# Weights and inputs laid out by the host as the chip wants them, and one scaling moved behind its load, in a two-layer hybrid decoder on eight cores

## The chip, the cores and the metric

The kernel runs on all 8 cores of one Trainium2 chip, one sequence of the batch per core. The metric is the device time of the slowest core, in microseconds (us). Most executions agree within 0.3%. Some fall into a slower state in which the cores of one die show a lower granted TensorE clock and the time is several per cent longer, whatever the kernel; those runs are left out of every comparison here, and only fast runs are compared with fast runs.

Engines are named as in the profile: PE is TensorE (matmuls and transposes), PEld its weight loads, DVE VectorE, ACT ScalarE, POOL GpSimd, SP SyncE. A kernel line is written L756.

## The reference, cut to what matters

```python
# D_MODEL 1024, BATCH 8, SEQ 2048, DEPTH 2, FFN_HIDDEN 2816, PLE_DIM 256
def even_mixer(x, w_in, w_out, conv_w, conv_b, ln_g, ln_b, pos):      # layer 0
    z = x @ w_in                                   # 1024 -> 5632
    q, k, v, u = jnp.split(z, [1536, 3072, 4608], axis=-1)
    ...                                            # rope on q, k; dilated window attention
    conv = conformer_conv(u, conv_w, conv_b, ln_g, ln_b)    # GLU, 31 taps, LN, SiLU
    return jnp.concatenate([attn, conv], axis=-1) @ w_out

def short_conv_mixer(x, w_in, conv_w, w_out): ...                     # layer 1

def reference(x, p, ...):
    for i in range(DEPTH):
        mix = even_mixer(...) if i % 2 == 0 else short_conv_mixer(...)
        x = layer_norm(DN_ALPHA * x + mix, ln_mix_g[i], ln_mix_b[i])
        x = layer_norm(DN_ALPHA * x + swiglu(x, ffn_w_in[i], ffn_w_out[i]), ln_ffn_g[i], ln_ffn_b[i])
        x = x + (p[i] @ ple_w_proj[i]) * jax.nn.sigmoid(x @ ple_w_gate[i])
    return x
```

All inputs are float32; the kernel computes its matmuls in bf16. A load from float32 in memory to a bf16 tile casts on the way, and in this kernel all of those are issued by POOL.

## The kernel before

`S.op`, `S.mm` and `S.dma` record an instruction with the tiles that it reads and writes; semaphores are derived from that. Every engine runs its own instructions in the order in which they were recorded.

Weights come through a ring of four tiles. A piece is 256 columns of a weight matrix, cut out of the row-major original in one or two loads:

```python
    def _wissue():
        while wq["issued"] < len(pieces) and wq["issued"] - 4 < wq["done"]:
            m = wq["issued"]
            i = m % 4
            fns = []
            for (src, co) in pieces[m]:
                n = src.shape[1]                                   # 128 or 256 columns
                fns.append(lambda e, src=src, co=co, n=n, i=i: e.dma_start(
                    out=ring[i][:, :, co:co + n], in_=src.rearrange("(kc p) n -> p kc n", p=128)))
            S.dma("pool", fns, ds_ring[i], writes=[r_ring[i]])
            wq["issued"] += 1
```

The start loads x by rows as float32, casts, transposes on PE, and after each four tiles of 128 tokens runs the GLU matmuls of the Conformer part for these 512 tokens. Two diagonal matrices for the convolution are built on POOL afterwards.

```python
    S.dma("sp", [... ropeC ..., ... ropeS ...], ds_misc, writes=[r_ropeC, r_ropeS])   # 2 MB
    for t in range(NT):
        S.dma("sp", [... x_tok[:, t, :] <- x_d[t * 128:(t + 1) * 128, :]], ...)
    ...
    for t in range(NT):
        if t + 2 < NT:
            p0_cast(t + 2)
        cb, r_cb = stg[t % 4]
        transpose_to(cb, r_cb, lambda t=t: xT[:, :, t * 128:(t + 1) * 128], r_xT[t // 4], 8,
                     "dve" if t % 2 == 0 else "act")
        if t % 4 != 3:
            continue
        ...                                        # GLU: 64 matmuls for this chunk
    # ... cut ...
    build_dg(0)
    build_dg(1)
```

The middle of the feed-forward part (four of the six groups of hidden columns). An output tile is 8 matmuls into PSUM and a DVE add that empties it:

```python
    def ffn_mid(l):
        S.dma("sp", [... lnp2 <- LN rows ...], ds_ln, writes=[r_lnp2])
        S.dma("pool", [... Wpg <- pwg_d[l] ..., ... Wpp <- pwp_d[l] ...], ds_ple, writes=[r_Wpg, r_Wpp])
        S.op("dve", lambda e: e.tensor_scalar_mul(out=Wpp[:], in0=Wpp[:], scalar1=0.5), rw=[r_Wpp])
        for t in range(NT):
            out_tile(0, t, False)
        for pi in range(1, len(FG) - 1):
            ...                                    # inproj tiles of group pi, 4 pieces
            load_wfo(l, pi + 1)
            for t in range(NT):
                out_tile(pi, t, False)
```

The tail is a software pipeline: round k works on tile k of the input projection, on tile k - 4 of the output, k - 5 of the layer norm, k - 6 of the transposes, k - 7 of the gate.

```python
    def ffn_tail(l, last, fill):
        for k in range(NT + 4 + 6):
            ...                                    # inproj(k % 4, k // 4)
            if ok(k - 4):
                out_tile(pi, k - 4, True)          # with LN statistics
            ln_apply(k - 5, lg, r_lnp2, lb, r_lnp2)
            if ok(k - 6):
                t = k - 6
                transpose_to(pbt[t % 2], r_pbt[t % 2], lambda t=t: pTt[t % 2][:], r_pTt[t % 2], 2, "dve")
                transpose_to(castt[t % 2], r_castt[t % 2], lambda t=t: x2T[t % 2][:], r_x2T[t % 2], 8, "dve")
            if ok(k - 5):
                p_load(l, k - 5)                   # 128 rows of p, 64 KB as bf16
            if ok(k - 7):
                p_main(l, k - 7)                   # x2T @ Wpg, tanh, pTt @ Wpp, gate, POOL add
            if ok(k - 5):
                cast_to(k - 5, castt[(k - 5) % 2], r_castt[(k - 5) % 2])       # ACT
            ...
```

The softmax here doesn't subtract the row's maximum and nothing guards it: scores larger than these inputs give would overflow.

## Time and profile before

| | before |
|---|---|
| median of 4 runs | 2335.0 us (2333.38 to 2335.57) |
| profiled execution, slowest core | 2333.9 us (core 3) |
| PE busy | 84% |
| DVE, POOL, ACT busy | 53%, 25%, 18% |
| granted PE clock, die 0 and die 1 | 0.938, 0.940 |
| software DMA packets | 154496 |

The chain of waits, the sums of the waits and the busy time by stretch are read in the prediction below. The two tails by stretch (columns: from:to, length, then busy time of PE, PEld, DVE, ACT and POOL with the number of instructions, PE clock, DMA share, GB/s):

```profile
1289.00:1512.00 223.00, 184.18 (x1018) 89.12 (x1017) 155.84 (x205) 57.91 (x65) 90.81 (x69) 0.93 0.12 15
2157.00:2334.00 177.00, 147.93 (x767) 69.55 (x765) 125.41 (x157) 39.39 (x44) 88.09 (x64) 0.94 0.18 54
```

Neither PE nor DVE fills these stretches, so they are held by waits between engines. The waits of PE from 2165 us to the end say which (us in all, times, longest):

```profile
PE ptb L455 <- DMA pbt<-p: 14.5, 6, 4.2
PE ptb L455 <- DVE x_tok L783: 6.9, 3, 2.7
PE ptb L455 <- ACT castt L500: 0.3, 1, 0.3
```

And the timeline at the head of this tail, where the first two tiles of the gate part come (start, length, engine, line, work, in brackets the idle time before it and what ended it):

```profile
2185.14 0.37 PE L455 MATMUL ptb<-ident,pbt 128*128 128x128 bf16 x2 [3.76 <-DMA pbt<-p]
...
2186.16 2.76 PE L774 MATMUL pd<-Wfo,hTf 128*128 128x512 bf16 x6
2193.13 0.37 PE L455 MATMUL ptb<-ident,pbt 128*128 128x128 bf16 x2 [4.21 <-DMA pbt<-p]
```

PE stands still for 8.0 us in all.

### The profile page before, as it was taken

Reading aid. Unit: us, or ns where it says so; the run is one execution under the profiler, and the core shown is the slowest. Engines: PE = TensorE matmul, PEld = TensorE weight load, DVE = VectorE, ACT = ScalarE, POOL = GpSimd, SP = SyncE. Lnnn points to the kernel's source line nnn. Section 1 sums busy time; section 2 is a strip of 40 time slices with the busy share of each in tenths; the row PEclk is TensorE's granted clock in tenths of the full one; section 3 lists DMA queues with packets and bytes.
Section 4 is the critical chain, followed back from the end, with each engine's and each line's share of the span. In section 5 each row is a group of like instructions: output and inputs, shape, how many; then the busy total and the mean of one; then the engine's idle time right before and its main releaser. Section 6 shows DMA issues by size and latency. Waiting matters only on the chain.

```text
span 2333.9 us, 27781 instructions; the slowest of 8 cores (2324.1 to 2333.9 us)
## 1 busy us (share of the span) xinstructions
PE 1950.2 (84%) x10046; PEld 939.2 (40%) x10046; DVE 1230.6 (53%) x1605; ACT 415.1 (18%) x629; POOL 586.9 (25%) x453
## 2 busy tenths in 40 slices
PE   3878787788853588699999897899897799999897
PEld 1434444345431243244444343444443344444443
DVE  1252665726735674333444676666883432444686
ACT  1203112231132221011001132211111011001122
POOL 1061633305410123010011254210332010100365
PEclk9999998999966799799999898999999899999899
DMA  9140201102045007352333003063217232232012
GB/s 191 33 47 12 28 9 20 18 11 28 10 55 162 0 1 90 46 54 25 40 41 41 4 8 32 22 80 38 29 18 87 39 46 28 37 40 32 23 62 79
DMA packets 163701, 97.30 MB, mean 42 GB/s; under 512 B 119280, under 2 KB 145904, under 8 KB 163312
## 3 DMA queue, kind: packets, MB, share of 16 engines
q0 software_dynamic: 154496, 63.97, 24.6%
q1 hardware_dynamic: 9072, 31.54, 4.2%
q8 instruction: 84, 1.38, 0.2%
q14 instruction: 49, 0.40, 0.1%
HBM read 151.08 MB, written 8.39 MB: 68 GB/s over the span
## 4 chain that ended last, share of the span: by engine, by line
PE 60%; DVE 18%; issue 8%; DMA 6%; ACT 5%; POOL 3%; DVEq 0%; SPq 0%; ACTq 0%; POOLq 0%
PE pd L750 24%; PE pd L774 12%; PE pd L943 6%; PE pd L853 4%; PE pd L630 3%; DMA x_tok<-x 2%; PE pd L736 2%; DVE rtmp L613 2%; DMA Wpp<-ple_w_proj 2%; DVE PT L661 2%; DVE rtmp L616 2%; DVE rtmp L610 2%; PE ptb L455 2%; DVE x_tok L492 1%; DVE UD L688 1%
## 5 line engine op out<-in xcount | busy, mean ns | idle before, releaser
L750 PE MATMUL pd<-xT,ring 128*128 128x512 bf16 x2816 | 620.6, 381 | 0.0
L750 PEld LDWEIGHTS pd<-xT,ring 128*128 128x128 bf16 x2816 | 275.8, 98 | 329.8 <-issue 6.4
L774 PE MATMUL pd<-Wfo,hTf 128*128 128x512 bf16 x1408 | 318.0, 385 | 47.6 <-DVE x_tok L779 47.6
L754 DVE TENSOR_TENSOR hTf<-pd,sgt 128x512 bf16<-128x512 f32 x176 | 121.7, 691 | 430.6 <-PE pd L750 407.2
L411 POOL DMA_DIRECT2D ring<-ffn_w_in x88 | 77.6, 890 | 665.5 <-PE pd L750 646.3
L753 ACT ACTIVATE sgt<-pd 128x512 f32<-128x512 f32 x176 | 104.7, 595 | 726.9 <-PE pd L750 726.9
L783 DVE TENSOR_TENSOR x_tok<-x_tok,pd 128x1024 f32<-128x1024 f32 x160 | 195.2, 1220 | 63.8 <-PE pd L774 54.9
L774 PEld LDWEIGHTS pd<-Wfo,hTf 128*128 128x128 bf16 x1408 | 139.0, 99 | 217.3 <-issue 56.5
L605 PE MATMUL pd<-xT,ring 128*128 128x512 bf16 x768 | 176.5, 384 | 30.8 <-DVE rtmp L616 29.0
L484 POOL TENSOR_SCALAR mvall<-mvall 128x1 f32<-128x1 f32 x64 | 64.6, 1009 | 465.3 <-DVE mvall L483 441.4
L943 PE MATMUL pd<-xT,ring 128*128 128x512 bf16 x768 | 170.7, 384 | 3.2 <-DMA ring<-odd_w_in 2.3
L620 POOL TENSOR_TENSOR qT<-rtmp,rtmp 128x512 bf16<-128x512 f32 x48 | 85.5, 1784 | 215.7 <-DVE rtmp L616 215.6
L661 DVE TENSOR_TENSOR PT<-PT,masks 128x256 bf16<-128x256 bf16 (+1 forms) x96 | 46.4, 483 | 161.3 <-ACT PT L658 161.3
L605 PEld LDWEIGHTS pd<-xT,ring 128*128 128x128 bf16 x768 | 72.9, 98 | 132.5 <-issue 54.7
L569 PE MATMUL pd<-hTc,dgb 128*128 128x512 bf16 x496 | 124.4, 387 | 0.0
L853 PE MATMUL pd<-Wpg,x2T 128*128 128x512 bf16 x512 | 123.2, 397 | 0.0
L455 PE MATMUL ptb<-ident,castt 128*128 128x128 bf16 x576 | 47.9, 233 | 80.6 <-ACT castt L500 54.1
L943 PEld LDWEIGHTS pd<-xT,ring 128*128 128x128 bf16 x768 | 75.3, 99 | 94.5 <-issue 7.8
L630 PE MATMUL pd<-ring,xT 128*128 128x256 bf16 x768 | 94.2, 284 | 22.2 <-DVE rtmp L616 22.2
L500 ACT ACTIVATE castt<-x_tok 128x1024 bf16<-128x1024 f32 x64 | 67.5, 1054 | 206.5 <-DVE x_tok L495 203.2
L869 POOL TENSOR_TENSOR x_tok<-x_tok,sigt 128x1024 f32<-128x1024 f32 x32 | 75.8, 2370 | 89.4 <-DVE sigt L867 72.0
L486 POOL TENSOR_TENSOR mvall<-mvall,cneg 128x1 f32<-128x1 f32 x64 | 95.3, 1490 | 9.5
(122 smaller groups left out, 2157.0 us busy)
## 6 DMA issues: line engine op xcount, KB each, us to landing
ring<-ffn_w_in POOLq DMA_DIRECT2D x88, 256.0 KB, 6.1
x_tok<-x SPq DMA_DIRECT2D x32, 512.0 KB, 6.6
ring<-even_w_in POOLq DMA_DIRECT2D x18, 512.0 KB, 7.8
Wfo<-ffn_w_out POOLq DMA_DIRECT2D x8, 1024.0 KB, 12.7
out<-x_tok SPq DMA_DIRECT2D x16, 512.0 KB, 2.7
Wpg<-ple_w_gate POOLq DMA_DIRECT2D x2, 2048.0 KB, 21.9
ring<-odd_w_in POOLq DMA_DIRECT2D x16, 256.0 KB, 7.9
Wfo<-ffn_w_out POOLq DMA_DIRECT2D x4, 768.0 KB, 9.8
```

Source lines behind the costliest of these rows:

```text
L455: fns = [lambda e, c=c, pt=pt: e.transpose(out=pt[:, c * 128:(c + 1) * 128], in_=src_bf[:, c * 128:(c + 1) * 128], identity=ident[:]) for ...
L486: S.op("pool", lambda e: e.tensor_tensor(out=mvall[:, t, 2:3], in0=mvall[:, t, 1:2], in1=cneg[:], op=ALU.pow), reads=[r_cneg], rw=[r_mvall ...
L569: fn = lambda e, tap=tap, bk=bk, j=j, tc=tc: e.matmul(bk, lhsT=dgb[j % 2][:, tap, :], rhs=hTc[:, j, tc * 512 + 2 + tap:tc * 512 + 2 + tap ...
L605: fns = [lambda e, d=d, bk=bk, w_=w_, h=h, tc=tc: e.matmul(bk, lhsT=w_[:, d, h * 128:(h + 1) * 128], rhs=xT[:, d, tc * 512:(tc + 1) * 512] ...
L630: fns = [lambda e, d=d, bk=bk, st0=st0, dil=dil, wv=wv: e.matmul(bk[:, 0:256], lhsT=xT[:, d, st0:st0 + 127 * dil + 1:dil], rhs=wv[:, d, :] ...
L750: S.mm([lambda e, d=d, bk=bk, o=o: e.matmul(bk, lhsT=slot[:, d, o:o + 128], rhs=xT[:, d, c * 512:(c + 1) * 512], start=(d == 0), stop=(d = ...
L753: S.op("act", lambda e: e.activation(out=sgt[k2][:], in_=bg, func=AF.Silu), reads=rg, writes=[r_sgt[k2]])
L754: S.op("dve", lambda e: e.tensor_tensor(out=hTf[:, fl, c * 512:(c + 1) * 512], in0=bu, in1=sgt[k2][:], op=ALU.mult), reads=ru + [r_sgt[k2] ...
L774: fns.append(lambda e, half=half, ff=ff: e.matmul(bD[:, half * 512:(half + 1) * 512], lhsT=hTf[:, ff, t * 128:(t + 1) * 128], rhs=Wfo[wb][ ...
L783: S.op("dve", lambda e: e.tensor_tensor(out=x_tok[:, t, :], in0=x_tok[:, t, :], in1=bD[:], op=ALU.add), reads=rD, rw=[r_xtok[t]])
L853: fns.append(lambda e, half=half, c=c: e.matmul(bG[:, half * 512:(half + 1) * 512], lhsT=x2T[k2][:, c, :], rhs=Wpg[:, c, half * 512:(half ...
L943: S.mm([lambda e, d=d, bk=bk, w_=w_, o=o: e.matmul(bk, lhsT=w_[:, d, o:o + 128], rhs=xT[:, d, c * 512:(c + 1) * 512], start=(d == 0), stop ...
```

## The change

Its intent is to have the host lay out what the chip otherwise rearranges, and to take three waits off the path:

- weights: 78 pieces, each packed by the host so that a partition's part is one contiguous run, one load instead of one or two;
- x a second time, transposed by the host, loaded with a cast straight into xT; rope tables only after it; one diagonal built at the start;
- p transposed by the host, 16 loads of 128 KB instead of 32 of 64 KB, no transposes of it on PE;
- Wpg, Wpp and their LN rows loaded after feed-forward group 1, the scaling by 0.5 done in group 3;
- the last two adds on DVE instead of POOL.

The other large weights (the output projections, the gate and the projection) are reordered by the host too, so that a partition's part is contiguous.

```diff
     def _wissue():
-        while wq["issued"] < len(pieces) and wq["issued"] - 4 < wq["done"]:
+        while wq["issued"] < min(len(PIECES), wq["lim"]) and wq["issued"] - 4 < wq["done"]:
             m = wq["issued"]
             i = m % 4
-            fns = []
-            for (src, co) in pieces[m]:
-                n = src.shape[1]
-                fns.append(... e.dma_start(out=ring[i][:, :, co:co + n], in_=src.rearrange(...)))
-            S.dma("pool", fns, ds_ring[i], writes=[r_ring[i]])
+            S.dma("pool", [lambda e, m=m, i=i: e.dma_start(out=ring[i][:], in_=wp_d[m])], ds_ring[i], writes=[r_ring[i]])
 ... cut: the loads of rope tables and of x by rows, casts and transposes at the start are removed ...
+    def xT_load(c):
+        S.dma("pool", [lambda e: e.dma_start(out=xT[:, :, c * 512:(c + 1) * 512], in_=xT_d[c])], ds_xT[c], writes=[r_xT[c]])
+    wq["lim"] = 1
+    _wissue()
+    xT_load(0)
+    wq["lim"] = len(PIECES)
     glu_slots = [wnext() for _ in range(4)]
+    for c in range(1, 4):
+        xT_load(c)
+    S.op("pool", ... dgb[1] = ident * ccw[:, 1, :] ...)
+    xT_landed = list(r_xT[3].ws.values())
 ... cut: GLU matmuls, unchanged ...
+    S.dma("sp", [... ropeC ..., ... ropeS ...], ds_misc, writes=[r_ropeC, r_ropeS], deps=xT_landed)
     build_dg(0)
-    build_dg(1)
     def ffn_mid(l):
-        S.dma("sp", [... lnp2 ...])
-        S.dma("pool", [... Wpg ..., ... Wpp ...], ds_ple, writes=[r_Wpg, r_Wpp])
-        S.op("dve", lambda e: e.tensor_scalar_mul(out=Wpp[:], in0=Wpp[:], scalar1=0.5), rw=[r_Wpp])
         for t in range(NT):
             out_tile(0, t, False)
 ... cut ...
             load_wfo(l, pi + 1)
+            if pi == 1:
+                S.dma("pool", [... Wpg ..., ... Wpp ...], ds_ple, writes=[r_Wpg, r_Wpp])
+                S.dma("sp", [... lnp2 ...])
+            if pi == 3:
+                S.op("dve", lambda e: e.tensor_scalar_mul(out=Wpp[:], in0=Wpp[:], scalar1=0.5), rw=[r_Wpp])
 ... cut: p_load takes two tiles at once from the transposed p ...
-        S.op("pool", lambda e: e.tensor_tensor(out=x_tok[:, t, :], in0=x_tok[:, t, :], in1=sg_[:], op=ALU.add),
+        S.op("dve" if l == 1 and t >= NT - 2 else "pool", lambda e: e.tensor_tensor(...),
 ... cut: in the tail ...
-                transpose_to(pbt[t % 2], r_pbt[t % 2], lambda t=t: pTt[t % 2][:], r_pTt[t % 2], 2, "dve")
                 transpose_to(castt[t % 2], r_castt[t % 2], lambda t=t: x2T[t % 2][:], r_x2T[t % 2], 8, "dve")
-            if ok(k - 5):
-                p_load(l, k - 5)
+            if ok(k - 5) and k % 2:
+                p_load(l, (k - 5) // 2)
 ... cut: the host code that packs and transposes ...
```

## The prediction

> **What bounds the kernel now.** I read the chain of waits first, because it names what ended last in each stage; then the waits, summed; then busy time by stretch, and the timeline where the two left a question. Columns of the chain: start, length (us), work.
>
> ```profile
> 7.34 18.29 DMA x_tok<-x
> ...
> 56.66 3.30 DMA x_tok<-x
> 63.81 3.46 PE pd L539 x8
> ...
> 129.06 6.82 POOL dgb L559
> ...
> 926.24 24.90 DMA Wpp<-ple_w_proj
> 953.20 25.09 PE pd L774 x104
> ...
> 1424.15 12.54 DMA pbt<-p
> ...
> 1797.02 22.48 DMA Wpp<-ple_w_proj
> ```
>
> Mostly the chain is PE matmuls (60% of the span by engine), but it leaves PE for a transfer at the start, once in each feed-forward stage, and often in the two tails. The waits (total us, times, longest) size this:
>
> ```profile
> PE ptb L455 <- DMA pbt<-p: 37.4, 12, 12.5
> ...
> DVE Wpp L828 <- DMA Wpp<-ple_w_proj: 52.2, 2, 27.3
> PE pd L774 <- DVE x_tok L779: 47.6, 2, 25.0
> ```
>
> The last two are one event. DVE multiplies Wpp by 0.5 as its first instruction of the stage, sits until the 2.6 MB of Wpg and Wpp have landed, and cannot empty PSUM; after three tiles PE stops. Busy time by stretch (core 3; PE, PEld, DVE, ACT, POOL, PE clock, DMA share, GB/s):
>
> ```profile
> 0.00:64.00 64.00, 22.00 (x129) 11.85 (x130) 9.54 (x18) 12.49 (x14) 8.80 (x17) 1.00 0.92 192
> 925.00:955.00 30.00, 5.02 (x20) 1.98 (x19) 3.77 (x4) 0.00 (x0) 1.96 (x3) 0.60 0.97 122
> 955.00:1290.00 335.00, 335.00 (x1546) 151.43 (x1545) 135.35 (x138) 35.82 (x60) 29.44 (x34) 1.00 0.34 35
> 1825.00:2170.00 345.00, 345.00 (x1600) 156.37 (x1599) 137.57 (x140) 38.21 (x64) 27.65 (x32) 1.00 0.28 33
> ```
>
> In the first 64 us the DMA engines are the bound (0.92 busy, PE 22 us). In 955 to 1290 and 1825 to 2170 PE is never idle, so faster weight loads are worth nothing there. So of the packing I count only the start; the rest of the gain comes from reordering.
>
> ```profile
> DMA packets 163701, 97.30 MB, mean 42 GB/s; under 512 B 119280, under 2 KB 145904, under 8 KB 163312
> ...
> q0 software_dynamic: 154496, 63.97, 24.6%
> ```
>
> The mean software packet writes 414 B and costs 24.6% x 2333.9 x 16 / 154496 = 59.5 ns of one engine.
>
> **What the Trainium skill says.** "DMA: Bandwidth & Descriptors", section "Why small descriptors are slow (HBM only)": each packet carries a fixed overhead. The trace agrees in direction: weight pieces with 256 B written per packet move about 90 GB/s per unit of DMA share, Wpg with 2 KB rows about 150 (932 to 951). Two rates give, as my estimate, t = 20.9 ns + 0.0963 ns per byte written; at 414 B that is 60.8, against 59.5 from the page. The same page, section "Anatomy of one DMA": a fixed cost of about 2 us a transfer; the 64 KB loads of p land in 2.4 us, so it agrees. "TensorE: Matmul & The Clock Gate", Part 1: a PE left idle for some 3.4 us restarts at half clock. It agrees: after the waits eight matmuls take 3.46 us, afterwards 1.73, so each long gap costs about 1.7 us more. "GPSIMD Engine Reference", section "Engine selection": two-input elementwise work is about 2x slower on GpSimd; here the final add takes 2.34 us on POOL and a like one 1.21 on DVE.
>
> **The change part by part.**
>
> 1. Start. Now 16 tiles of x are loaded as f32 beside 4.2 MB of weights in small packets and 2 MB of rope tables, cast, and transposed on PE with four breaks. The GLU matmuls start at 43.1 and end at 120.1. Afterwards x arrives transposed by casting loads, in the order piece 0, xT0, pieces 1 to 3, xT1 to xT3; the rope tables wait for xT3. By the estimate xT (1 KB rows written) moves 137 GB/s, 7.7 us a chunk, and a packed piece (4 KB rows if runs merge) 158 GB/s, 3.3 us. First issue at 3.07 as now, plus 2 fixed, plus 3.3 + 7.7: xT0 at 16.1. Pieces 1 to 3 at 19.4, 22.7, 26.0; xT1, xT2, xT3 at 33.7, 41.3, 49.0. A chunk of GLU is 64 matmuls in 13.8 us (four times 3.45), the first 1.7 more: it ends at 31.6, the second runs 33.7 to 47.5, the third to 61.3, the fourth to 75.1. The last two find their data waiting. I take 76.5 for the end: gain 43.6.
>
> 2. One of two diagonal builds (POOL L559, 6.8 us each) moves from after GLU to the idle POOL at the start. At 129 to 136 it holds up the rope adds; DVE then waits 8.56 us and PE 6.74. With one build DVE waits about 1.8: gain 6.8.
>
> 3. Wpg, Wpp and their LN rows are loaded after the second feed-forward group, the scaling is done two groups later. The gaps of 25.0 and 22.6 go, with two cold restarts of 1.7: gain 51.0. The new place has 27.6 us of output matmuls plus a 55.25 us input group before anything else depends on it, and a DMA share near a third.
>
> 4. First tail. It runs from 1289 to 1512, 223 us. What remains for PE: 12 input tiles x 3.45, 16 output tiles x 1.30, 32 transposed tiles x 0.45, 16 gates with their projection x 4.31, 5 odd-layer units x 5.18 = 41.4 + 20.8 + 14.4 + 69.0 + 25.9 = 171.5. The 16 transposes of p (0.23 each, 3.7) vanish. The waits on pbt here (22.9) and on DVE pTt for a transpose bank (10.2) vanish as such, but the start must still wait about 2 us twice for the LN chain plus cold restarts (7), the last castd stays (5.5), and in some four rounds without an input tile DVE needs about 8 us against PE's 6.5 (7 to 10). 171.5 + 7 + 5.5 + 10 = 194: gain 29. It includes the 12.5 us wait: p sat behind three weight pieces; now it is issued two rounds ahead.
>
> 5. Second tail, 2156.8 to 2333.9, 177.1 us. PE work 131.2 + 7.2 for one set of transposes = 138.4. I keep 12 of the 21.7 us of PE waits, 3 of 5 for cold restarts and 6.1 of the 7.4 after the last matmul (the final add moves to DVE: 1.2 saved). That is 159.5, and rounding towards caution 161: gain 16.
>
> 6. Fewer and cheaper issues on POOL and the late odd-layer piece (PE waits 2.3): gain 3.
>
> Sum: 43.6 + 6.8 + 51.0 + 29 + 16 + 3 = 149.4. From 2335.0 that is 2185.6; I predict 2186 us.
>
> **The rivals.** First, the tails become bound by DVE. In favour: in 2266 to 2310 DVE has hardly a gap. Against: the first tail has PE waits that only p's transposes cause, and a round with an input tile needs 8.2 to 8.7 of DVE against 9.4 to 10.0 of PE. If half of parts 4 and 5 is lost: 2208. Second, the first load stays the bound: the casting loads get no faster than about 100 GB/s, or queue out of order. Then xT3 lands at about 66 and GLU ends near 82 to 84: 2192. It can't be much worse, for the last chunk needs only 13.8 us after its data. Third, the moved 2.6 MB load runs into the weight pieces and PE waits in a later group: for 10 us each, 2206. Against: one piece is due per 13.8 us and takes 3.3 to 6. Fourth, the good side: DVE runs ahead through freed banks and both tails follow PE: 2172.
>
> **Range and chances.** The Wpp wait and the diagonal build (58) are nearly certain. The start can miss by about 7, the tails together by 18, the small part by 3. With a little more room on the slow side the range is 2168 to 2208. Faster by over 2% means under 2288, which needs less than a third of the sum: 0.985. Within 2%: 0.012. Slower: 0.003.
>
> **What would show it.** Right: first GLU matmul near 16, last near 76; no wait on Wpp and an unbroken PE in the feed-forward stages; no wait of PE on p; one build of 6.8 us after GLU; software packets down from 154496 to about 20,000 to 30,000; the first tail near 194 us and the second near 161. Wrong: gaps between GLU chunks of more than 3 us past the first, PE waiting for a ring piece or Wfo after the moved load, or PE waits in the tails that have moved from p to castt by the same length. The prediction fails if the tails keep more than 30 us of the waits on p under another name, or if x lands later than 60.

## The result, and the profile after

| | before | after |
|---|---|---|
| median | 2335.0 us (4 runs); 2335.8 (13, one of them slow) | 2187.0 us (9 runs, 2184.4 to 2200.1) |
| ratio of fast runs | | 0.9374 (95%: 0.9358 to 0.9391) |
| profiled execution | 2333.9 us, core 3 | 2184.9 us, core 5 |
| PE busy | 1950.2 us, 84% | 1917.7 us, 88% |
| POOL busy | 586.9 us | 499.8 us |
| PE clock, die 0 and 1 | 0.938, 0.940 | 0.955, 0.954 |

A ratio is the mean time of one kernel's fast runs over the mean of the other's fast runs of the same rounds, so not quite the ratio of the medians quoted. Two runs of the changed kernel, 2198.7 and 2200.1 us, count as fast although one die shows a clock of 0.944 instead of 0.955 and is about 15 us longer; the other eight lie between 2184.4 and 2187.6 us, mean 2186.4. The change is faster by 6.3%. The result is correct, and so is that of every experiment below.

**Where the time came from.** I took the start of the same first matmul of each stage in both traces and subtracted.

| stretch | before us | after us | gain us | predicted |
|---|---|---|---|---|
| start to the first rope matmul | 122.2 | 77.9 | 44.3 | 43.6 |
| rope to the first V matmul | 38.9 | 32.1 | 6.8 | 6.8 |
| rest of attention | 560.3 | 559.3 | 1.0 | part of the 3 |
| mixer, layer 0 | 180.9 | 180.8 | 0.1 | 0 |
| first output group, both layers | | | 27.6 + 24.5 = 52.1 | 51.0 |
| four middle groups, each layer | 310.8 | 310.8 | 0 | 0 |
| first tail | 222.9 | 192.8 | 30.1 | 29 |
| odd layer and its mixer | | | 3.7 + 0.5 | rest of the 3 |
| second tail | 177.1 | 166.6 | 10.5 | 16 |

The gains add to 149.1 with rounding; the profiled spans differ by 149.0. The chain that ended last after the change (start, length, work) shows the new path:

```profile
6.25 28.16 DMA xT<-xT
...
74.52 1.74 PE pd L523 x8
77.94 1.90 PE pd L587 x8
...
870.93 27.63 PE pd L756 x128
898.55 55.25 PE pd L732 x256
```

The GLU matmuls (L520, L523) end at 76.3. The first output group (L756, 128 matmuls) is one unbroken piece of 27.63 us with the next input group right behind it; before, a 24.90 us transfer of Wpp stood in that place. No Wpp is left anywhere in this chain. The start in the timeline:

```profile
18.02 3.57 PE L520 MATMUL pd<-xT,ring 128*128 128x512 bf16 x8 [18.02 <-DMA xT<-xT]
...
34.65 1.67 PE L520 MATMUL pd<-xT,ring 128*128 128x512 bf16 x7 [0.44 <-DMA xT<-xT]
```

PE starts at 18.0, waits 0.44 us for the second chunk of x, and never again in this stage. Between these two starts 16.6 us pass, in which the second chunk and three pieces, 2.62 MB as written, come in: 158 GB/s. The page on packets:

```profile
DMA packets 27185, 93.05 MB, mean 43 GB/s; under 512 B 3248, under 2 KB 9392, under 8 KB 25264
...
q0 software_dynamic: 20288, 68.16, 19.1%
```

Software packets fell from 154496 to 20288, but the time for which they hold an engine only from 24.6% to 19.1% of the span, which is 574 us before (0.246 x 2333.9) and 417 after. Nearly eight times fewer packets bought about a quarter of the time, because each is larger and because x, 4 MB as bf16, now comes by this queue. Issuing became cheaper too: a ring load occupied POOL 890 ns, 134 times; now 557 ns, 78 times, and that is most of POOL's 87 us.

What PE waits for now, in all (us, times, longest), and what of it falls into the first tail (from 1209 us) and into the second (from 2018 us):

```profile
PE ptb L445 <- ACT castt L490: 81.0, 35, 10.7
...
PE pd L520 <- DMA xT<-xT: 18.5, 2, 18.0
```

```profile
PE ptb L445 <- ACT castt L490: 11.3, 6, 5.9
```

```profile
PE ptb L445 <- ACT castt L490: 17.1, 10, 5.9
```

Waits on p and on Wpp are gone as named; in the second tail there is a single name now, castt, with 17.1 us where p, the add and castt had 21.7. In the first, castt has 11.3 us where p and the copies of its transposes (pTt) had 22.9 + 10.2 = 33.1. In both tails together castt is named for 28.4 us, and was for 0.3 before. The stretches after:

```profile
899.00:1209.00 310.00, 310.00 (x1438) 140.52 (x1437) 119.55 (x125) 35.82 (x60) 11.54 (x21) 1.00 0.27 46
1209.00:1402.00 193.00, 175.83 (x986) 86.34 (x984) 153.61 (x189) 57.46 (x65) 84.50 (x59) 0.97 0.11 17
2018.00:2185.00 167.00, 143.84 (x738) 67.06 (x735) 124.58 (x144) 39.58 (x44) 79.59 (x54) 0.96 0.18 57
```

In the middle groups PE is busy for every microsecond, before as after, so cheaper weight loads could buy nothing there, and did not. In the first tail PE lost 8.4 us of work, but 30 us of time; in the second PE lost 4.1 of work (and with it the clock rose from 0.94 to 0.96) and 10.5 of time.

The head of the second tail is the instructive spot:

```profile
2045.10 0.61 PE L445 MATMUL ptb<-ident,castt 128*128 128x128 bf16 x8 [2.23 <-ACT castt L490]
2045.54 1.46 PE L756 MATMUL pd<-Wfo,hTf 128*128 128x512 bf16 x6
2052.93 1.01 PE L445 MATMUL ptb<-ident,castt 128*128 128x128 bf16 x8 [5.92 <-ACT castt L490]
```

These two waits are 8.15 us; the two on p in the same place were 8.0. The load of p had only been the last of two: before, the casts ended at 2183.5 and 2191.3, 1.7 and 1.8 us ahead of the matmuls that waited for p. So the time gained here is not the 8 us of the waits, and it is not zero either. The first gate matmul starts 35.6 us after the first matmul of the tail (2053.7 - 2018.1), and before it was 37.6 (2194.2 - 2156.6). The waits are as long as before, but PE's work between them is shorter: after the wait of 3.76 us six output matmuls took 2.76 us, after the one of 2.23 us they take 1.46. The order on ACT tells why castt is late: the cast of tile 0 is ahead of the SiLU of an input tile, waits for the layer norm and runs at 2043.9; the SiLU comes at 2044.9 though its matmuls were done by about 2041.6; the product on DVE waits for it (1.74 us), the add of the next output tile stands behind that product on DVE, and so the next norm and the next cast (2051.7) are late.

Later, in the rounds that have no input tile, DVE sets the pace:

```profile
2126.36 1.22 DVE L765 TENSOR_TENSOR x_tok<-x_tok,pd 128x1024 f32<-128x1024 f32 x1
...
2133.50 1.21 DVE L765 TENSOR_TENSOR x_tok<-x_tok,pd 128x1024 f32<-128x1024 f32 x1
```

A round takes 7.14 us (2133.50 - 2126.36), without a gap between DVE's eight instructions, while PE's share of it is about 6.1; PE waits 0.8 to 0.9 us on castt in each.

### The profile page after: what moved, and what is told of

Same layout as the page of the kernel before. It is cut to its first block, busy times and chain, and to the rows that moved or that the text cites. A ratio compares the mean times of both kernels' runs of the same rounds, so it can differ in the third digit from the quotient of the medians.

```text
span 2184.9 us, 27087 instructions; the slowest of 8 cores (2176.9 to 2184.9 us)
## 1 busy us (share of the span) xinstructions
PE 1917.7 (88%) x9854; PEld 923.7 (42%) x9854; DVE 1216.1 (56%) x1559; ACT 399.4 (18%) x613; POOL 499.8 (23%) x383
## 3 DMA queue, kind: packets, MB, share of 16 engines
q0 software_dynamic: 20288, 68.16, 19.1%
## 4 chain that ended last, share of the span: by engine, by line
PE 64%; DVE 19%; issue 7%; ACT 5%; POOL 2%; DMA 2%; DVEq 0%; ACTq 0%; POOLq 0%
PE pd L732 27%; PE pd L756 13%; PE pd L925 6%; PE pd L835 4%; PE pd L612 3%; PE pd L718 3%; DVE rtmp L595 2%; DVE PT L643 2%; DVE x_tok L482 2%; DVE rtmp L598 2%; DVE rtmp L592 2%; DVE UD L670 1%; PE pd L552 1%; DMA xT<-xT 1%; DVE x_tok L485 1%
## 5 line engine op out<-in xcount | busy, mean ns | idle before, releaser
L756 PE MATMUL pd<-Wfo,hTf 128*128 128x512 bf16 x1408 | 310.7, 379 | 0.0
L406 POOL DMA_DIRECT2D ring<-w_pack x78 | 43.3, 557 | 876.5 <-PE pd L732 652.7
L756 PEld LDWEIGHTS pd<-Wfo,hTf 128*128 128x128 bf16 x1408 | 137.5, 98 | 164.8
L445 PE MATMUL ptb<-ident,castt 128*128 128x128 bf16 x512 | 41.7, 228 | 81.2 <-ACT castt L490 81.0
L670 DVE TENSOR_TENSOR UD<-pd,UD 128x512 f32<-128x512 f32 x64 | 67.9, 1060 | 57.1 <-PE pd L658 21.1
```

The source lines that it names most:

```text
L756: fns.append(lambda e, half=half, ff=ff: e.matmul(bD[:, half * 512:(half + 1) * 512], lhsT=hTf[:, ff, t * 128:(t + 1) * 128], rhs=Wfo[wb][ ...
```

## The experiments

Twelve kernels, all with five rounds. Where I give the cost of an edit against the changed kernel, it is the mean of the fast runs less 2186.4 us, the mean of the changed kernel's eight runs without a slowed die; the changed kernel itself was run again (E12) and stands at 2186.0. One fast run of E6 and one of E10 again have a die with a lower clock, and are named there. About 1 us of such a difference is not to be trusted.

### E12: the changed kernel once more

No edit; it runs beside E9 to E11 on the same chip.

> The changed kernel itself, on the chip of the three runs beside it, as their measure: 2185 to 2189 us, ratio to before 0.935 to 0.939.

Measured: fast mean 2186.0 us (median of all five runs 2186.8, one of them slow), ratio 0.9365 (0.9344 to 0.9386). The result repeats.

### E1: the early load and the early scaling put back

```diff
 def ffn_mid(l):                       # in the changed kernel
+    S.dma("pool", [... Wpg ..., ... Wpp ...]); S.dma("sp", [... lnp2 ...])
+    S.op("dve", ... Wpp *= 0.5 ...)
     for t in range(NT):
         out_tile(0, t, False)
-            if pi == 1: ... loads ...
-            if pi == 3: ... Wpp *= 0.5 ...
```

> The changed kernel with Wpg, Wpp, their LN rows and the scaling of Wpp put back to the head of each feed-forward stage. Theory (DVE, in order, waits at the scaling and PE runs out of PSUM): two PE gaps of about 22 us each with a cold restart, 42 to 50 us slower than the changed kernel, 2229 to 2237 us. Rival (with large packets the old place costs nothing): at most 10 us slower, below 2197.

Measured: median 2230.2 us, ratio 0.9555 (0.9542 to 0.9569): about 44 us slower than the changed kernel. The chain and the waits:

```profile
872.43 22.41 DMA Wpp<-ple_w_proj
...
1705.06 21.20 DMA Wpp<-ple_w_proj
```

```profile
PE pd L756 <- DVE x_tok L761: 41.0, 2, 21.1
```

Both transfers are back on the path with 41 us of PE waits. That is less than the 47.6 of before; E5 shows that packed pieces alone bring this down to 39.2.

### E2: the early load alone, the scaling left late

```diff
 def ffn_mid(l):                       # in the changed kernel
+    S.dma("pool", [... Wpg ..., ... Wpp ...]); S.dma("sp", [... lnp2 ...])
     for t in range(NT):
         out_tile(0, t, False)
-            if pi == 1: ... loads ...
             if pi == 3: ... Wpp *= 0.5 ...          # stays
```

> The changed kernel with only the loads put back to the head of the stage; the scaling stays two groups later. Theory (the wait of the in-order DVE is the cause, not the traffic): within 2 us of the changed kernel, 2185 to 2189. Rival (the 2.6 MB load itself holds up weight pieces or Wfo): 10 to 25 us slower.

Measured: the fast runs lie between 2186.6 and 2187.1, ratio 0.9369 (0.9356 to 0.9383). That is the changed kernel's time, and no PE wait on x_tok is left in the feed-forward part. The load may stand early or late; it does not matter. The 44 us of E1 are all due to one DVE instruction that sits at the head of its queue until 2.6 MB have landed, with the adds that empty PSUM behind it. The rival, that the transfer itself holds up the weight pieces, is refuted.

### E3: in the kernel before, only the scaling moved

```diff
 def ffn_mid(l):                       # in the kernel before
-    S.op("dve", lambda e: e.tensor_scalar_mul(out=Wpp[:], in0=Wpp[:], scalar1=0.5), rw=[r_Wpp])
     for t in range(NT):
         out_tile(0, t, False)
 ...
             load_wfo(l, pi + 1)
+            if pi == 3:
+                S.op("dve", lambda e: e.tensor_scalar_mul(out=Wpp[:], in0=Wpp[:], scalar1=0.5), rw=[r_Wpp])
```

> The kernel before with one thing changed: the scaling of Wpp is issued in the fourth output group, the loads stay. Theory: both gaps of 25.0 and 22.6 us and two cold restarts go, 51 us faster than before, 2281 to 2288. Rival (traffic of the load with small packets beside it holds PE): only 10 to 25 us faster, 2310 to 2325.

Measured: three fast runs, 2279.9, 2282.5 and 2282.8 us (the median of all six, 2340.5, is made by slow ones); ratio 0.978 (0.9761 to 0.9798), 53 us less than before. The trace of the full change gives 52.1 for the same place. One line moved is a third of the whole gain.

### E4: p by rows again, transposed on PE

```diff
 # in the changed kernel
+                transpose_to(pbt[t % 2], r_pbt[t % 2], lambda t=t: pTt[t % 2][:], r_pTt[t % 2], 2, "dve")
                 transpose_to(castt[t % 2], r_castt[t % 2], lambda t=t: x2T[t % 2][:], r_x2T[t % 2], 8, "dve")
-            if ok(k - 5) and k % 2:
-                p_load(l, (k - 5) // 2)
+            if ok(k - 5):
+                p_load(l, k - 5)
```

> The changed kernel with p loaded by rows again, one tile at a time, and transposed on PE. Theory: both tails get back nearly all that they gained (30.1 and 10.5 us between the traces) less the final add (1.2) and less the shorter queue ahead of p in the first tail (three packed pieces land sooner): 32 to 40 us slower than the changed kernel, 2219 to 2227. Rival (the tails are bound by DVE and the LN chain, p only named last): under 15 us slower.

Measured: median 2221.6 us, ratio 0.9519 (0.9505 to 0.9532), 35.4 us over the changed kernel. The second tail takes 177.5 us instead of 166.6, the first 217.1 instead of 192.8, so 10.9 and 24.3 us. The PE waits, and the timeline at the head of the first tail:

```profile
PE ptb L446 <- DMA pbt<-p: 39.0, 15, 7.7
```

```profile
1238.57 0.37 PE L446 MATMUL ptb<-ident,pbt 128*128 128x128 bf16 x2 [3.90 <-DMA pbt<-p]
...
1246.46 0.37 PE L446 MATMUL ptb<-ident,pbt 128*128 128x128 bf16 x2 [4.31 <-DMA pbt<-p]
```

So p on PE costs 35 of the 40.6 us that both tails gained; the other 5.8 of the first tail fit E5, where packed pieces alone take 6.2 us off it. (With p off PE this part is gone: rows again, E6, leave the first tail as long as in the changed kernel.) At the head PE's idle time is the same with p and without: 3.90 + 4.31 = 8.2 us here, and 8.15 in the changed kernel (2.23 + 5.92, in the first tail as in the second). It does not follow that p costs nothing there. The first gate matmul starts 37.6 us after the first matmul of the tail with p (1247.5 - 1209.9) and 35.6 without (1244.8 - 1209.2). So at the head the named wait was worth 2.0 us and not its 8; the rest of it only changed its name, and the larger gain lies in the rounds after the head.

E4 undoes two things at once: the transposes of p on PE, and the load that is issued two rounds ahead instead of one. Which of them counts more was not separated. In the chain before, the load that ended the second wait at the head of the second tail was issued at 2190.53, just when an operation of the layer norm on POOL (2188.99, 1.54 us) had ended, so it also waited for its turn on POOL; a load of p by rows, issued a round earlier, is the rival that no run tested.

### E5: in the kernel before, only the weight pieces packed

```diff
 # in the kernel before
-            for (src, co) in pieces[m]: ... e.dma_start(out=ring[i][:, :, co:co + n], in_=src.rearrange(...))
-            S.dma("pool", fns, ds_ring[i], writes=[r_ring[i]])
+            S.dma("pool", [... e.dma_start(out=ring[i][:], in_=wp_d[m])], ds_ring[i], writes=[r_ring[i]])
```

> The kernel before with one thing changed: the 78 weight pieces are packed, one contiguous load each. Theory (packing is worth something only where a transfer is waited for: the start about 9 us, the queue ahead of Wpg twice about 4, the queue ahead of p about 5, the late odd-layer piece about 2): 18 to 26 us faster than before, 2309 to 2318. Rival (shorter loads and issues help in all stages): 40 us faster or more, under 2296.

Measured: four fast runs, mean 2311.2 us (the median of all eight, 2373.0, is made by slow ones); ratio 0.9898 (0.9875 to 0.9921), 23 us less than before. The total is in the range that I had written, but it is distributed otherwise. The first rope matmul starts at 117.9 instead of 122.2, a gain of 4.3 where I expected about 9. By stage the trace has 3.9 us in each first output group, 6.2 in the first tail and 2.6 in the odd layer; the other 4.5 of the 25.4 between the two profiled spans are spread over attention, mixers and second tail. The larger ones lie where the queue is shorter ahead of loads that something waits for:

```profile
PE pd L770 <- DVE x_tok L775: 39.2, 2, 20.8
PE ptb L451 <- DMA pbt<-p: 34.1, 15, 6.2
```

The wait behind Wpp fell from 47.6 to 39.2 and the longest on p from 12.5 to 6.2: fewer and larger packets stand ahead of them. In the full change both waits are removed anyway, so this part of packing's worth exists only without the other parts.

### E6: the changed kernel with pieces by rows

```diff
 # in the changed kernel
-            S.dma("pool", [... e.dma_start(out=ring[i][:], in_=wp_d[m])], ds_ring[i], writes=[r_ring[i]])
+            for (a, w) in cols:
+                fns.append(... e.dma_start(out=ring[i][:, :, co:co + w], in_=src[:, a:a + w].rearrange("(kc p) n -> p kc n", p=128)))
+            S.dma("pool", fns, ds_ring[i], writes=[r_ring[i]])
```

> The changed kernel with the weight pieces read by rows from the original arrays again (512 B or 1 KB runs). Theory (only the start and the late odd-layer piece wait for pieces): pieces of 5.8 us instead of 3.3 put xT0 2.5 us and xT1 about 11 us later, with the odd-layer piece 12 to 18 us slower than the changed kernel, 2199 to 2205, and no new PE wait in the feed-forward stages. Rival (packing carries much of the gain): 30 us slower or more.

Measured: fast runs 2199.2, 2213.5 and 2201.0 us (the median of all seven, 2380.5, is made by slow ones); ratio 0.9441 (0.9407 to 0.9475). That is 18 us over the changed kernel by the means. But the run of 2213.5 has die 0 at a clock of 0.944 against 0.955 on die 1, and 16 us longer; without it the cost is 13.7 us, and by the two profiled spans it is 12.7. At the start PE now waits for pieces:

```profile
35.14 3.45 PE L528 MATMUL pd<-xT,ring 128*128 128x512 bf16 x8 [2.27 <-DMA ring<-even_w_in]
```

The first rope matmul starts at 85.2 instead of 77.9. So of the 44.3 us gained at the start, packing alone gives 4.3 (E5), the other edits of the start without packing 37.0 (122.2 - 85.2), and 3.0 come only with both. The slowest core of this trace also spends 4.9 us more in the attention part, but that is mostly scatter between cores: in one execution the eight cores differ there by 5.4 us in the changed kernel and by 7.2 in this one, and their medians differ by 1.7. The wait for the late odd-layer piece, which I had expected, comes back on seven of the eight cores, with 0.7 to 3.2 us; in the changed kernel no core waits more than 0.3 for one. In the feed-forward part no new wait appears: a piece lands 5.9 us (median) after its issue, and PE works 13.8 us with each.

### E7: rope tables loaded first again

```diff
 # in the changed kernel
+    S.dma("sp", [... ropeC ..., ... ropeS ...], ds_misc, writes=[r_ropeC, r_ropeS])     # at the start
 ...
-    S.dma("sp", [... ropeC ..., ... ropeS ...], ds_misc, writes=[r_ropeC, r_ropeS], deps=xT_landed)
```

> The changed kernel with the two rope tables (2.1 MB) loaded at the start instead of after the last chunk of x. Theory (the start is bound by the DMA engines, whatever queue feeds them): first GLU matmul and end of GLU about 7 us later, 5 to 8 us slower, 2192 to 2195. Rival (another queue, so free): within 2 us of the changed kernel.

Measured: fast mean 2192.2 us (the median of all six, 2221.2, includes slow ones), ratio 0.9389 (0.9365 to 0.9412), 6 us over the changed kernel. In its trace the first GLU matmul starts at 24.20 us instead of 18.02, the first rope matmul at 83.6 instead of 77.9. At the start, 2 MB that nobody needs yet cost 6.2 us at the first GLU matmul; put behind the last chunk they land 6.8 and 9.0 us after issue and delay nothing.

### E8: the second diagonal built after GLU again

```diff
 # in the changed kernel
-    S.op("pool", ... dgb[1] = ident * ccw[:, 1, :] ...)     # at the start
 ...
     build_dg(0)
+    build_dg(1)
```

> The changed kernel with both diagonal builds on POOL after GLU again. Theory (rope adds wait behind the second build, DVE and then PE behind them): 6.8 us slower, 2193 to 2195. Rival (this stage has slack): under 2 us.

Measured: fast mean 2193.1 us, ratio 0.9392 (0.9371 to 0.9412), 6.8 us over the changed kernel; the first V matmul starts at 116.6 instead of 110.1. That is one build, 6.8 us, as the prediction had it.

### E9: x2T copied out of PSUM by ACT instead of DVE

```diff
 # in the changed kernel
-                transpose_to(castt[t % 2], r_castt[t % 2], lambda t=t: x2T[t % 2][:], r_x2T[t % 2], 8, "dve")
+                transpose_to(castt[t % 2], r_castt[t % 2], lambda t=t: x2T[t % 2][:], r_x2T[t % 2], 8, "act")
```

> The changed kernel with one operand of the tails changed: the transposed tile x2T leaves PSUM through ACT instead of DVE. Theory (the rounds of the tails without an input tile are bound by DVE, whose 7.13 us hold no gap against 6.06 of PE): 0.6 us less in each of some 8 rounds of the second tail and some 4 of the first, 4 to 8 us faster than the changed kernel, 2179 to 2183. Rival (the rounds are bound by the chain output tile, LN, cast, transpose): within 1.5 us, or slower, since the ACT copy takes about 1.0 us against 0.68.

Measured: fast mean 2179.7 us, ratio 0.9338 (0.9316 to 0.9359), 6.4 us less than E12 on the same chip. The same place in the timeline as shown for the changed kernel:

```profile
2123.30 1.21 DVE L765 TENSOR_TENSOR x_tok<-x_tok,pd 128x1024 f32<-128x1024 f32 x1
...
2130.03 1.21 DVE L765 TENSOR_TENSOR x_tok<-x_tok,pd 128x1024 f32<-128x1024 f32 x1
```

A round shrinks from 7.14 to 6.73 us (the next to 6.53) and the second tail from 166.6 to 162.2. The first tail is 2.8 us shorter too, and the odd layer behind it 1.4 longer (116.7 against 115.3, medians of the cores). Taking 0.68 us of copy from DVE makes the rounds shorter: there DVE was indeed the bound, the first rival of the prediction.

### E10: the cast one round later on ACT, behind the SiLU

```diff
 # in the changed kernel, in the loop of the tail
+            if ok(k - 6):
+                cast_to(k - 6, castt[(k - 6) % 2], r_castt[(k - 6) % 2])     # ahead of the transposes, behind inproj's SiLU
 ...
-            if ok(k - 5):
-                cast_to(k - 5, castt[(k - 5) % 2], r_castt[(k - 5) % 2])
```

> The changed kernel with the cast of a tile issued one round later, behind the SiLU of that round on ACT instead of ahead of it. Theory (PE's waits of 2.2 and 5.9 us at the head of each tail come from the SiLU queued behind a cast that waits for LN): about 2 us less at the head of each tail, 2 to 5 us faster than the changed kernel, 2182 to 2185. Rival (LN itself is what lasts): within 1 us, or slower where the cast now starts later.

Measured: fast runs 2181.2, 2184.5, 2185.0 and 2194.7 us, ratio 0.9366 (0.9337 to 0.9396): as a total inconclusive. The run of 2194.7 has die 1 at a clock of 0.945 against 0.955 on die 0; the other three have a mean of 2183.5, 2.5 us less than E12, but differ by 3.8 themselves. The trace says more. The second wait at the head of the first tail, and the first one at the head of the second tail:

```profile
1242.63 1.01 PE L445 MATMUL ptb<-ident,castt 128*128 128x128 bf16 x8 [4.09 <-ACT castt L490]
...
2043.86 1.01 PE L445 MATMUL ptb<-ident,castt 128*128 128x128 bf16 x8 [2.51 <-ACT castt L490]
```

The head of the second tail waits 2.51 + 2.26 = 4.8 us instead of 8.15, its first gate matmul comes 33.4 us after the start of the tail instead of 35.6, and that tail takes 163.0 us instead of 166.6. In the first tail the second wait is 4.09 us instead of 5.92 and the first gate matmul comes at 33.8 instead of 35.6, but at the end of that tail only 0.8 us of it are left. So part of the head's wait, 3.4 of 8.15 us in the second tail (2.2 in time) and 1.8 in the first, was the SiLU standing behind the cast; the rest remains, and I read it as the chain of norm, cast and transpose itself, which no run took apart.

### E11: E9 and E10 together

```diff
 # in the changed kernel: both edits above
+            if ok(k - 6): cast_to(k - 6, ...)      # ahead of the transposes
-                transpose_to(castt[t % 2], ..., 8, "dve")
+                transpose_to(castt[t % 2], ..., 8, "act")
-            if ok(k - 5): cast_to(k - 5, ...)
```

> Both of the last two together. If both theories hold and add: 6 to 12 us faster than the changed kernel, 2175 to 2181.

Measured: five fast runs, 2177.4 to 2179.1, mean 2178.7 us; ratio 0.9335 (0.9314 to 0.9356), 7.3 us less than E12. This is the best version, 0.3% ahead of the changed kernel and 6.7% ahead of the kernel before. On top of E9 the later cast is worth 1.0 us, not its 3.6 us of the second tail: what E9 takes from DVE and what the later cast takes from the head overlap, and how was not taken apart.

## Why the prediction was right, point by point

The predicted time was 2186, the range 2168 to 2208, and the median came out at 2187.0. Six steps make the sum of 149.4 against 149.0 in the traces. Most held singly; one was mis-sized, and small surpluses of the others made up for it.

1. **Start: right, 44.3 for 43.6.** xT0 landed at 17.9 instead of 16.1 and xT1 at 34.4 instead of 33.7, but from then on PE ran through and ended at 76.25 for a predicted 76.5, because the gap of 2.1 us that I had kept ahead of the second chunk was only 0.44. The rival of a load-bound start did not come about. E6 and E7 show that each ingredient counts: pieces by rows cost 7.3 us here, early rope tables 5.7. (One reading under the estimate was a little off: from 932 to 951 us Wpg moves 149 GB/s at a DMA share of 1.03, so 145 per unit and not 150.)

2. **One diagonal build: right.** 6.8 by the trace, 6.8 by undoing it (E8).

3. **The wait behind Wpp: right in size and in mechanism.** 52.1 for 51.0; E1, E2 and E3 show that DVE's order was the cause and not the transfer. The rival that the moved load collides with weight pieces is refuted from both sides: wherever the load stands, no PE wait on a piece appears. In the changed kernel Wpp takes longer to land than it does in E1 (27.9 us against 21.8), and nobody notices: it is issued at 956 us and scaled at 1120.

4. **First tail: right in the sum, 192.8 us for 194; its terms were not.** Undoing p alone (E4) costs 24.3 us of these 30. For the head the prediction kept 7 us, low clock included: the two waits there are 8.15, and PE is busy 175.8 us instead of the 171.5 of work, so another 4.3 go to low clock, here and later. For the rounds without an input tile it kept 10: the waits on castt after the head are 11.3 - 8.15 = 3.2. That these two errors nearly cancel was luck.

5. **Second tail: the term that was mis-sized.** Predicted 161, measured 166.6: 10.5 us gained, not 16. The step that failed was "I keep 12 of the 21.7 us of PE waits". 17.1 remained, and at most 4.9 instead of 3 for restarts at low clock (166.6 less 138.4 of PE work, 17.1 of waits and 6.2 after the last matmul, so by difference). I had treated the 8.0 us on p at the head as removable in part. The trace after and E4 show that castt keeps PE idle there for as long as p did, and that the head as a whole became only 2.0 us shorter. The prediction's own sign for being wrong, waits that move from p to castt, did occur: in both tails together castt is named for 28.4 us now and was for 0.3 before, close to the 30 at which the prediction was to fail. What saved it is that all waits of PE on p, its copies, the add and castt in the tails had been 33.1 + 21.7 = 54.8 us, so about half of them did go. E9 shows the rest of the error: in rounds without an input tile DVE is the bound, as I had seen for the first tail but not counted as its own term in the second.

6. **The small part: 5.2 for 3** (1.0 in attention, 3.7 in the odd layer, 0.5 in its mixer). The 1.0 is within the scatter of the cores (5.4 us). In the odd layer packing alone (E5) gives 2.6, and rows (E6) bring the wait for its late piece back; the rest is not separated.

The error of -5.5 in the second tail was balanced by +0.7, +1.1, +1.1 and +2.2 in the others, so the exact total flatters the working a little.

What one change is worth depends on the others, so the parts as run do not have to add up: undoing one at a time costs 44 (scaling), 35 (p), 14 (packing, from the two undisturbed runs), 7 (build) and 6 us (rope tables), 106 together. The largest part without an experiment of its own is the arrival of x in transposed form; E5 and E6 together give it, with the order of loads and the cheaper start around it, 37 us in the trace.

## What to carry to other kernels

An instruction that waits for a transfer at the head of an in-order engine holds up everything behind it: move the consumer, and look where it stands in its engine's order, before touching the transfer. Before crediting a removed wait, ask what becomes ready just behind it; a profile names the last one only, and a second chain close behind it gives most of the time back (6 of 8 us at the head here). And compare when the next stage starts, not only the sums of the waits. Larger packets pay where a transfer is waited for, here at the start, in the first tail and in the odd layer (E5), and not in stages that PE already fills.

## What the Trainium skill lacked or had wrong

- "DMA: Bandwidth & Descriptors" has no rate for loads that cast float32 to bf16, which is what this kernel lives on. The runs show about 90 GB/s written per unit of DMA share at 256 B written per packet, about 145 at 2 KB rows, and 158 GB/s measured over 16.6 us at the start of the changed kernel.
- The same page, section "Anatomy of one DMA — SWDGE (gpsimd) path", calls descriptor generation small and variable. For POOL it is a cost to count: 890 ns for a ring load by rows, 557 ns for a packed one, in all about 119 us before (134 x 890 ns) and 43 after. The fit of that section, 2.0 us and bytes / 436e3, gives as an estimate 2.3 us for 128 KB; the transposed p lands 3.0 us after issue, of which 0.64 are POOL's own.
- "SBUF — State Buffer", section "Who interferes with whom", lacks nothing here; it has right what I failed to use: a DVE instruction with two SBUF inputs contends with a GpSimd instruction that reads SBUF. In the timeline of the changed kernel the masking of a 128x256 tile lasts 5.95 us where the median of this line is 0.42, and ends 0.14 us after the diagonal build on POOL:

```profile
232.44 6.81 POOL L542 TENSOR_TENSOR dgb<-ident,ccw 128x3968 bf16<-128x3968 bf16 x1 [8.72 <-PE pd L552]
233.44 5.95 DVE L643 TENSOR_TENSOR PT<-PT,masks 128x256 bf16<-128x256 bf16 x1 [0.88 <-ACT PT L640]
```

- "TensorE: Matmul & The Clock Gate", Part 1, puts the fall of the clock after an idle window of some 3.4 us. The length of one wait does not decide it here: in E10 eight transposes took 1.01 us after a wait of only 2.51 us, and 0.61 after one of 2.26, while in the changed kernel they took 0.61 after waits of 3.23 and 3.87 us (at 748 and 844 us). The page says that the window is free-running, that is, not tied to the waits; whether this accounts for the cases was not tested. Who counts the waits above 3.4 us does not count the restarts.
